# Weight rooms whose contents start 0, 16, 32 or 48 bytes in, by turns

## The chip, the cores and the metric

The kernel runs as one program on one core of a Trainium2 chip. The metric is the device time of that core in microseconds (us). Three runs of the kernel before gave 1257.59 us (median; 1257.32 to 1260.47).

A core has a matrix engine (TensorE, PE in the profile), a vector engine (VectorE, DVE), an activation engine (ScalarE, ACT), GpSimd (POOL) and SyncE (SP), which issues the DMAs. All of them work on SBUF, an on-chip memory of 128 partitions; a tile is a room with the same byte address in every partition. A matrix multiplication on PE takes two instructions: a weight load (LDWEIGHTS, shown as the engine PEld) puts the 128x128 stationary operand into the array, and a MATMUL streams the moving operand through it, one column after the other, into a PSUM bank. Both read SBUF. The weight load of the next MATMUL runs while the present MATMUL streams.

## The reference, cut to what matters

The kernel computes two decoder layers on 512 tokens of 1024 channels, each with a token mixer and a gated feed-forward network (hidden width 2816), in float32:

```
for i in range(2):
    hn = rmsnorm(h, norm_g[i, 0]) * (1 + scale) + shift        # scale, shift, gate from c @ ada_w[i, 0]
    m = s5_mixer(hn, ...) if i == 0 else fox_mixer(hn, ...)    # state space; forgetting attention
    h = h + gate * m
    hn = rmsnorm(h, norm_g[i, 1]) * (1 + scale) + shift        # from c @ ada_w[i, 1]
    a, b = split(hn @ ffn_w_up[i], 2)
    a = conv_b + sum(shifted(a, 2 - t) * conv_w[t] for t in range(3))
    h = h + gate * ((silu(a) * b) @ ffn_w_down[i])
return rmsnorm(h, final_g)
```

Most of the arithmetic is matrix products of activations with weights: 1024x1024 (three in the first mixer, four in the second), 1024x5632 and 2816x1024 in each network.

## The kernel before, in words

Channels lie on the partitions, tokens along the free dimension. A product is made in tiles: 128 output channels times 512 tokens in a PSUM bank (tile `mmp`), summed over blocks of 128 input channels (index k).

To keep float32 precision with the one-pass format float32r, each operand is stored as two rounded parts, high and low. `put_parts` makes them: ACT writes the high part (line 241), DVE subtracts it from the source and writes the low part (line 242). Each block k of a product is then three MATMULs (`mms`, line 258): high weights with the high activations, high weights with the low activations, low weights with the high activations. In an instruction's name the moving operand stands first: `mmp<-a_hi,w_lo` streams `a_hi` through the weights `w_lo`.

Weights come from HBM by `raw` (a DMA on SP's queue into a tile `raw`). `split` takes two tiles `w_hi` and `w_lo` from a pool, calls `put_parts` and returns them; `weights` does that for all blocks of one tile of output channels, in one to two splits. The rooms of `w_hi` and `w_lo` are five each (`WB`), and are used in rotation in `wpool`. The last output tiles of a network (two in the first, four in the second) take theirs from the network's own pool instead. `quarters`, in the second network, replaces a pair of products by seven smaller ones on halves (MATMULs of 256 columns, line 506); it rounds sums of weights the same way through its local `parts`. `load` inside `fox_values` splits the attention's value weights; there the weights are the moving operand (line 1275). In the second network, `sums` rounded by `form` serve as moving operands under the names `w_hi` and `w_lo` too; they lie in the network's pool.

The moving operands of the other products are `a_hi`, `a_lo` (normalized activations, one fixed room for all sub-layers), `zhi`, `zlo` (first mixer), `v` (second mixer, holding the attention's output) and `ghi`, `glo`: the gated product of a network, in groups of 11 blocks (first network, two groups through the same two rooms) or of 6 and 5 blocks (second network, four groups).

Where the rooms lie, as the program is built (bytes past a multiple of 64; every block k within a room is a multiple of 64 bytes further, so all blocks of a tile share this number):

| tile | before | with the change |
|---|---|---|
| `w_hi`, `w_lo` in `wpool` | 32 | 32, 48, 0, 16 by turns |
| `w_hi`, `w_lo` in a network's pool, as weights | 0 | 0, 16, 32, 48 by turns; those of `quarters` that hold `a22` stay at 0 |
| `a_hi`, `a_lo`, `zhi`, `zlo`, `v` | 32 | 32 |
| `ghi`, `glo`, first network | 0 | 16 (first group), 48 (second group) |
| `ghi`, `glo`, second network | 0 | 0 |
| rounded `sums` as moving operands | 0 | 0 |
| `raw` | 32 | 32 |

The rooms of `wpool` are 4096 bytes apart before and 4160 with the change, so that neighbouring rooms then differ by 64 bytes when counted past a multiple of 512. Before, all ten rooms lie 480 past a multiple of 512, as `a_hi` and `a_lo` do; `zhi`, `zlo` and `v` lie 32 past one, `ghi` and `glo` 384.

The order of the instructions on each engine is settled when the program is built. The scheduler places a tile's instructions as rooms come free.

Of the kernel before, what the change touches and what calls it, by code (L numbers as in the profile page):

```python
# [8 lines left out]
F32 = mybir.dt.float32  # L9
F32R = mybir.dt.float32r  # L10
# [7 lines left out]
P = 128  # L18
D = 1024
KT = D // P  # L20
S = 512
# [14 lines left out]
NEG = -1.0e30  # L36
HALVES = (slice(0, S // 2), slice(S // 2, S))
RAW, WB = 3, 5

GROUPS = (11, 11)  # L40
QGROUPS = (6, 5, 6, 5)
# [14 lines left out]
class Trunk:  # L56
# [6 lines left out]
    def __init__(self, tc, io, ctx):  # L63
        self.tc, self.nc, self.io, self.ctx = tc, tc.nc, io, ctx
        nc = self.nc
        pool = lambda name, bufs, **k: ctx.enter_context(tc.tile_pool(name=name, bufs=bufs, **k))
        self.const = pool("const", 1)
        self.act = pool("act", 1)
        self.wpool = pool("wpool", 3)
        self.tmp = pool("tmp", 2)  # L70
        self.small = pool("small", 2)
        self.dram = pool("dram", 1, space=DRAM)
        self.mm = pool("mm", 4, space=PSUM)
        self.aux = pool("aux", 4, space=PSUM)
        self.bg = []
        self.acc = None
        self.pending = None

        self.first = self.load_pack("first", FIRST)
        self.c = self.first["c"]  # L80
        self.ones = self.const.tile([P, P], F32, name="ones")
        nc.vector.memset(self.ones, 1.0)
        self.sc = self.const.tile([P, KT], F32, name="sc")
        nc.scalar.activation(self.sc, self.c, AF.Silu)
        self.sc32 = self.const.tile([P, KT, 32], F32, name="sc32")

        self.sel = self.const.tile([P, 6], F32, name="sel")
        nc.gpsimd.memset(self.sel, 0.0)
        for q in range(4):
            for c in (q, 4 + q % 2):  # L90
                nc.gpsimd.memset(self.sel[32 * q:32 * q + 1, c:c + 1], 1.0)
        self.par = [self.const.tile([P, 24], F32, name=f"par{i}") for i in range(4)]
        self.ga = [self.const.tile([P, KT], F32, name=f"ga{i}") for i in range(4)]
# [132 lines left out]
    def finish_norm(self, n=NORM_AFTER):  # L226

        if self.pending and n >= NORM_AFTER:
            with self.tc.issue_after(self.last_mm.ins):
                self.pending()  # L230
            self.pending = None

    def split(self, src, shape, pool=None, bufs=WB):

        hi, lo = ((pool or self.wpool).tile(shape, F32R, name=n, bufs=bufs) for n in ("w_hi", "w_lo"))
        self.put_parts(hi, lo, self.raw(shape, src))
        return hi, lo

# [5 lines left out]
    def weights(self, w, nk, *pool):  # L244

        out = []
        n8 = -(-nk // 8)
        for q in range(n8):
            a, n = q * nk // n8, (q + 1) * nk // n8 - q * nk // n8
            hi, lo = self.split(w[:, a:a + n, :], [P, n, P], *pool)  # L250
            out += [(hi[:, j, :], lo[:, j, :]) for j in range(n)]
        return out
# [217 lines left out]
    def quarters(self, pool, l, f, x, finish):  # L470

        nc = self.nc
        H, N = KT // 2, S // 2
        t1, t2 = HALVES
        a, b = (self.raw([P, KT, P], self.io["w_up"][l][2 * f + j]) for j in range(2))
        a11, a12, a21, a22 = a[:, :H], a[:, H:], b[:, :H], b[:, H:]
        c, d = (pool.tile([P, 2, H, P], F32, name="sums", bufs=2) for _ in range(2))
        sub = lambda o, u, v, op=ALU.subtract: nc.vector.tensor_tensor(o, u, v, op)
        w = {}

        def parts(src, names, *where):
            hi, lo = ((where[0] if where else self.wpool).tile(
                [P, len(names) * H, P], F32R, name=n, tag=(where[1] + n if where else n), bufs=1 if where else WB
            ) for n in ("w_hi", "w_lo"))
            self.put_parts(hi, lo, src)
            for j, n in enumerate(names):
                w[n] = hi[:, j * H:(j + 1) * H], lo[:, j * H:(j + 1) * H]

        parts(a, ("a11", "a12"))
        sub(c[:, 0], a21, a22, ALU.add)  # L490
        sub(c[:, 1], c[:, 0], a11)
        parts(c.rearrange("p n k m -> p (n k) m"), ("s1", "s2"))
        sub(d[:, 1], a11, a21)
        sub(d[:, 0], a12, c[:, 1])
        parts(d.rearrange("p n k m -> p (n k) m"), ("s4", "s3"))
        parts(a22, ("a22",), pool, "e")
        quarter = lambda k, t: tuple(v[:, k * H:(k + 1) * H, t] for v in x)
        xs = {"b11": quarter(0, t1), "b21": quarter(1, t1), "b22": quarter(1, t2)}
        for n, v in self.tx.items():
            xs[f"t{n}"] = v  # L500

        def times(o, wn, xn, first=True):
            (whi, wlo), (xhi, xlo) = w[wn], xs[xn]
            for k in range(H):
                for n, (wt, xt) in enumerate(((whi, xhi), (whi, xlo), (wlo, xhi))):
                    self.last_mm = nc.tensor.matmul(  # L506
                        o, wt[:, k], xt[:, k], start=(first and k == 0 and n == 0), stop=(k == H - 1 and n == 2),
                        skip_group_check=True,
                    )

        def copy(o):
            t = self.tmp.tile([P, N], F32, name="nm_h", bufs=4)
            nc.scalar.activation(t, o, AF.Copy)  # L513
            return t

        p1, p5 = (self.mm.tile([P, S], F32, name="mmp")[:, :N] for _ in range(2))
        p2, p4 = (self.aux.tile([P, S], F32, name="aux")[:, :N] for _ in range(2))
        oa, ob = (self.tmp.tile([P, S], F32, name="nm_t") for _ in range(2))
        times(p1, "a11", "b11")
        c1 = copy(p1)  # L520
        times(p5, "s1", "t1")
        c5 = copy(p5)
        times(p2, "a12", "b21")
        sub(oa[:, t1], p2, c1, ALU.add)
        times(p1, "s2", "t2", False)
        c2 = copy(p1)
        times(p5, "s4", "b22", False)
        sub(oa[:, t2], p5, c2, ALU.add)
        finish(2 * f, oa, slice(0, S))
        times(p4, "a22", "t4")  # L530
        c4 = copy(p4)
        times(p1, "s3", "t3", False)
        sub(ob[:, t2], p1, c5, ALU.add)
        sub(ob[:, t1], p1, c4)
        finish(2 * f + 1, ob, slice(0, S))

    def ffn(self, i, l, x, nxt, ticks=0, plain=None):

        nc, tc = self.nc, self.tc
        with tc.tile_pool(name=f"ffn{l}", bufs=1, reuse_waits="tile") as pool:  # L540
# [6 lines left out]
            keep, g = {}, {}  # L547

            def gated(m, ps, cols):
                f = m // 2  # L550
                if m % 2 == 0:
                    t = pool.tile([P, S], F32, name="conv", bufs=2 if plain else 3)
                    nc.scalar.activation(t, ps, AF.Identity, bias=cb[:, f:f + 1], scale=cw[:, 2, f:f + 1])
                    for d in (1, 2):
                        nc.vector.scalar_tensor_tensor(  # L555
                            t[:, d:], ps[:, :S - d], cw[:, 2 - d, f:f + 1], t[:, d:], op0=ALU.mult, op1=ALU.add
                        )
                    nc.scalar.activation(t, t, AF.Silu)  # L558
                    keep[f] = t
                    return  # L560
                t = keep.pop(f)
                nc.vector.tensor_tensor(t, t, ps, ALU.mult)
                q = sum(f >= n for n in first[1:])
                j = f - first[q]
                if not j:
                    tag = f"{q % 2}" if plain else ""
                    g[q] = [pool.tile([P, groups[q], S], F32R, name=n, tag=n + tag) for n in ("ghi", "glo")]
                hi, lo = g[q]
                self.put_parts(hi[:, j, :], lo[:, j, :], t)

# [157 lines left out]
class S5(Trunk):  # L728
# [34 lines left out]
    def s5_params(self, pool, tp, prm, stats):  # L763
# [19 lines left out]

        logs = [], []
        y = self.inv_root(stats, NB, log=logs[0])
        self.s5_turns(pool, co, si, logs[1])
        in_turn(*logs)
        yield y

# [41 lines left out]
        e.mul(m, m, self.mag8)  # L831
        yield last.ins

    def s5_turns(self, pool, er, ei, log):

        nc = self.nc
        H = G // 2
        LB = B.bit_length() - 1
        self.turn = pool.tile([P, LB, 3, H], F32, name="s5_turn")
        tmp = pool.tile([P, 2, 2, H], F32, name="s5_turn0")  # L840
        for k in range(LB + 2):
            o = self.turn[:, k - 2] if k >= 2 else tmp[:, k % 2]
            c, s = o[:, 0], o[:, 2 if k >= 2 else 1]
# [176 lines left out]
    def s5(self, i, nxt):  # L1020
# [5 lines left out]
        with ExitStack() as stack:  # L1026
# [3 lines left out]
            with ExitStack() as start:  # L1030
# [11 lines left out]
                with tc.manual_schedule(engines={ENG.PE, ENG.Activation, ENG.DVE, ENG.SP}):  # L1042
# [47 lines left out]
                    for k in range(KT):  # L1090
                        last_mm = nc.tensor.matmul(
                            col, w[0][:, k, :], self.par[i][:, k:k + 1], start=(k == 0), stop=(k == KT - 1)
                        )
                    shifted = self.small.tile([P, 1], F32, name="u_shift")
                    nc.scalar.activation(shifted, col, AF.Copy)
                    first = self.tmp.tile([P, L, B], F32, name="uf", tag="nm_t")
                    nc.scalar.activation(first, ps.rearrange("p (b j) -> p j b", j=L), AF.Identity, bias=shifted)
# [111 lines left out]
class Kernel(S5):  # L1209
# [32 lines left out]
    def fox_values(self, pool, x):  # L1242
# [9 lines left out]
        def load(q):  # L1252

            src = self.io["fox_v"][q - 1] if q else self.io["fox_vf"]
            n, step = (W, 4) if q else (W + NH, 3)
            out = []
            for a in range(0, KT, step):
                j = min(step, KT - a)
                hi, lo = self.split(src[:, a:a + j, :], [P, j, n])
                out += [(hi[:, i, :], lo[:, i, :]) for i in range(j)]  # L1260
            return out
# [267 lines left out]
```

## Time and profile before

| what | value |
|---|---|
| median of three runs | 1257.59 us (1257.32 to 1260.47) |
| span of the profiled execution, first to last instruction | 1254.6 us |
| mean granted TensorE clock | 0.995 |
| PE busy | 1234.3 us (98% of the span), 7464 MATMULs |
| PEld, DVE, ACT, POOL busy | 82%, 72%, 45%, 5% |
| PE's share of the chain that ended last | 94% |

The profiled execution's own time is its span, 1254.6 us; the median of the runs, which is taken with what lies around the span, is 3.0 us above it. In the profile a row of a group gives line, engine, operation, the tiles' names and sizes, the count, then busy time, mean duration and idle time before. MATMULs are pipelined: the next one starts before the end that the record gives, so the distance between starts is what one MATMUL costs PE, and the duration in the record is longer.

### The profile page before, as it was taken

How to read it: one execution, taken by the hardware profiler on the slowest of the kernel's cores; microseconds unless marked ns; L12 is line 12 of the kernel's file. 1: busy time of each engine (PE TensorE's matmuls, PEld its weight loads, DVE VectorE, ACT ScalarE, POOL GpSimd, SP SyncE). 2: the span in 40 equal slices, each digit the busy share in tenths (PEclk: the TensorE clock that was granted, in tenths of full speed). 3: DMA queues.
4: the chain of work that ended last, by engine and by line, in shares of the span. 5: the costliest groups of instructions: out<-in, count | busy, mean ns of one | idle time of the engine just before them, and what ended most of it. 6: DMA issues, size and time to landing. Idle time of an engine off the chain costs nothing.

```text
span 1254.6 us, 19342 instructions
## 1 busy us (share of the span) xinstructions
PE 1234.3 (98%) x7464; PEld 1024.5 (82%) x7464; DVE 897.5 (72%) x1610; ACT 565.8 (45%) x1043; POOL 57.5 (5%) x103
## 2 busy tenths in 40 slices
PE   7999999999999999999999999999999999999997
PEld 2566678898878778788799888878989999999987
DVE  7878887578765647666457467765899888887855
ACT  3543445334332233333334456654365555554543
POOL 0000000000000000000000224331000000000000
PEclk9999999999999999999999999999999999999999
DMA  9678667237744736545413433321213332332331
GB/s 364 231 227 259 205 196 244 99 103 234 236 137 148 236 118 221 168 147 165 141 49 103 149 117 131 133 94 53 85 60 101 120 119 82 106 118 88 102 84 68
DMA packets 73067, 183.22 MB, mean 146 GB/s; under 512 B 23079, under 2 KB 25471, under 8 KB 71951
## 3 DMA queue, kind: packets, MB, share of 16 engines
q1 hardware_dynamic: 72687, 181.46, 45.3%
q8 instruction: 59, 0.97, 0.3%
q10 hardware_dynamic: 288, 0.52, 0.1%
q14 instruction: 33, 0.27, 0.1%
HBM read 175.04 MB, written 6.92 MB: 145 GB/s over the span
## 4 chain that ended last, share of the span: by engine, by line
PE 94%; DVE 2%; DMA 1%; ACT 1%; issue 0%; SPq 0%; DVEq 0%; ACTq 0%
PE mmp L258 58%; PE mmp L506 10%; PE mmp L1110 4%; PE aux L506 4%; PE mmp L1275 2%; PE aux L916 2%; PE mmp L1139 2%; PE aux L1417 2%; PE aux L1400 1%; PE mmp L181 1%; PE aux L1005 1%; PE aux L997 1%; PE aux L1370 1%; PE mmp L1080 1%; PE mmp L1050 1%; PE aux L955 1%
## 5 line engine op out<-in xcount | busy, mean ns | idle before, releaser
L241 ACT ACTIVATE w_hi<-raw 128x1024 fp32r<-128x1024 f32 (+4 forms) x197 | 181.8, 927 | 258.2 <-PE mmp L258 211.5
L242 DVE TENSOR_TENSOR w_lo<-raw,w_hi 128x1024 fp32r<-128x1024 f32 (+4 forms) x197 | 210.1, 1070 | 92.0 <-ACT w_hi L241 88.2
L258 PE MATMUL mmp<-a_hi,w_hi 128*128 128x512 f32 (+1 forms) x624 | 235.8, 380 | 2.2 <-ACT a_hi L394 1.5
L258 PE MATMUL mmp<-a_hi,w_lo 128*128 128x512 f32 (+1 forms) x624 | 233.3, 374 | 0.0
L258 PE MATMUL mmp<-a_lo,w_hi 128*128 128x512 f32 (+1 forms) x624 | 232.7, 373 | 0.0
L258 PE MATMUL mmp<-ghi,w_hi 128*128 128x512 f32 (+1 forms) x394 | 147.2, 374 | 0.0
L258 PE MATMUL mmp<-glo,w_hi 128*128 128x512 f32 (+1 forms) x394 | 146.8, 373 | 0.0
L258 PE MATMUL mmp<-ghi,w_lo 128*128 128x512 f32 (+1 forms) x394 | 146.7, 372 | 0.0
L258 PEld LDWEIGHTS mmp<-a_hi,w_hi 128*128 128x128 f32 x624 | 117.1, 188 | 25.9 <-issue 2.6
L258 PEld LDWEIGHTS mmp<-a_hi,w_lo 128*128 128x128 f32 x624 | 117.5, 188 | 21.1 <-DVE w_lo L242 0.3
L258 PEld LDWEIGHTS mmp<-a_lo,w_hi 128*128 128x128 f32 x624 | 117.6, 188 | 19.3
L324 DVE SCALAR_TENSOR_TENSOR h<-mmp,par,h 128x512 f32<-128x512 f32 (+1 forms) x74 | 49.9, 678 | 63.9 <-PE mmp L258 63.6
L258 PEld LDWEIGHTS mmp<-ghi,w_lo 128*128 128x128 f32 x394 | 74.4, 189 | 14.1
L258 PEld LDWEIGHTS mmp<-ghi,w_hi 128*128 128x128 f32 x394 | 74.5, 189 | 13.5
L258 PEld LDWEIGHTS mmp<-glo,w_hi 128*128 128x128 f32 x394 | 74.5, 189 | 13.5
L209 DVE SCALAR_TENSOR_TENSOR ada_acc<-ada_raw,sc,ada_acc 128x1024 f32<-128x1024 f32 x49 | 62.8, 1282 | 26.6 <-DMA ada_raw<-in_ada_w 26.3
L506 PE MATMUL mmp<-w_hi 128*128 128x256 f32 x216 | 60.7, 281 | 0.2 <-ACT nm_h L513 0.2
L506 PE MATMUL mmp<-w_hi,w_lo 128*128 128x256 f32 x216 | 60.5, 280 | 0.0
L506 PE MATMUL mmp<-w_lo,w_hi 128*128 128x256 f32 x216 | 60.5, 280 | 0.0
L558 ACT ACTIVATE conv<-conv 128x512 f32<-128x512 f32 x44 | 27.5, 629 | 66.7 <-DVE conv L555 66.3
L1110 PE MATMUL mmp<-a_x,raw 128*128 128x512 f32 x112 | 54.9, 627 | 0.0
L242 DVE TENSOR_TENSOR w_lo<-sums,w_hi 128x1024 fp32r<-128x1024 f32 x40 | 48.9, 1222 | 3.8 <-ACT w_hi L241 3.7
(298 smaller groups left out, 2487.9 us busy)
## 6 DMA issues: line engine op xcount, KB each, us to landing
raw<-in_w_up SPq DMA_DIRECT2D x88, 512.0 KB, 3.4
ada_raw<-in_ada_w SPq DMA_DIRECT2D x56, 512.0 KB, 4.4
raw<-in_ada_w SPq DMA_DIRECT2D x40, 512.0 KB, 6.3
raw<-in_w_down SPq DMA_DIRECT2D x32, 384.0 KB, 3.2
raw<-in_w_down SPq DMA_DIRECT2D x32, 320.0 KB, 3.0
nf<-nfd SPq DMA_DIRECT2D x8, 1152.0 KB, 5.7
raw<-in_fox_qk SPq DMA_DIRECT2D x16, 512.0 KB, 3.7
h<-in_x SPq DMA_DIRECT2D x8, 512.0 KB, 5.6
```

Source lines behind the costliest of these rows:

```text
L209: nc.vector.scalar_tensor_tensor(acc, w, self.sc[:, k:k + 1], acc, op0=ALU.mult, op1=ALU.add)
L241: nc.scalar.activation(hi, src, AF.Copy)
L242: nc.vector.tensor_tensor(lo, src, hi.bitcast(F32), ALU.subtract)
L258: self.last_mm = self.nc.tensor.matmul(o, wt, xt[:, cols], start=(k == 0 and n == 0), stop=(k == nk - 1 and n == 2),)
L324: self.nc.vector.scalar_tensor_tensor(self.h[:, m, cols], ps, self.par[i][:, 16 + m:17 + m], self.h[:, m, cols], op0=ALU.mult, op1=ALU.add,)
L506: self.last_mm = nc.tensor.matmul(o, wt[:, k], xt[:, k], start=(first and k == 0 and n == 0), stop=(k == H - 1 and n == 2), skip_group_che ...
L558: nc.scalar.activation(t, t, AF.Silu)
L916: nc.tensor.matmul(ps[g2][:, j, cols], x[rows, a + j, r].rearrange("p c j -> p (c j)"), self.rr[rows, planes, q, :], start=(j == 0 and r = ...
L1110: nc.tensor.matmul(ps, w[m][:, k, :], x[:, k], start=(k == 0), stop=(k == KT - 1))
L1139: nc.tensor.matmul(gps[m], wt, xt[:, k], start=(k == 0 and part == 0 and xt is yhi), stop=(k == KT - 1 and part == 1))
L1275: self.last_mm = nc.tensor.matmul(ps[q, b][:, :n], xt[:, k, tb], wt, start=(k == 0 and i == 0), stop=(k == KT - 1 and i == 2),)
L1417: nc.tensor.matmul(pv[:, c * P:], self.v[:, hp, k, r].rearrange("p t d -> p (t d)"), pp[:, r, c + 3 * k:NB + 3 * k, :].rearrange("p b t -> ...
```

## The change

`PAD` is 16 elements (64 bytes). A new method `room` takes a tile that is 64 bytes longer than needed and returns a view that begins `off` elements into it. `turn_skew` steps an offset through 4, 8, 12, 0 elements: 16, 32, 48, 0 bytes. `split` and the `wpool` part of `parts` in `quarters` use that offset for both `w_hi` and `w_lo`; `weights`, `quarters` and `load` step it once per call. The rooms of the gated product in the first network begin 4 elements (first group) or 12 elements (second group) in. Two small tiles, `s5_turn0` (512 bytes) and `u_shift` (4 bytes), move from pools that live long into the pool of the start (`tp`). The instructions, their sizes and their order on the five engines are the same as before; in the first mixer one wait of DVE on a DMA's semaphore is attached to a later write of the tile `ua` than before.

```diff
+PAD = 16
...
+        self.skew = 0
...
+    def room(self, pool, shape, name, off, **k):
+
+        n = math.prod(shape[1:])
+        t = pool.tile([P, n + PAD], F32R, name=name, **k)
+        return t[:, off:off + n].rearrange("p (a b) -> p a b", b=shape[2])
+
+    def turn_skew(self):
+        self.skew = (self.skew + 4) % PAD
+
     def split(self, src, shape, pool=None, bufs=WB):
 
-        hi, lo = ((pool or self.wpool).tile(shape, F32R, name=n, bufs=bufs) for n in ("w_hi", "w_lo"))
+        hi, lo = (self.room(pool or self.wpool, shape, n, self.skew, bufs=bufs) for n in ("w_hi", "w_lo"))
         self.put_parts(hi, lo, self.raw(shape, src))
         return hi, lo
...
     def weights(self, w, nk, *pool):
 
         out = []
+        self.turn_skew()
...
+        self.turn_skew()
+
         def parts(src, names, *where):
-            hi, lo = ((where[0] if where else self.wpool).tile(
-                [P, len(names) * H, P], F32R, name=n, tag=(where[1] + n if where else n), bufs=1 if where else WB
-            ) for n in ("w_hi", "w_lo"))
+            shape = [P, len(names) * H, P]
+            if where:
+                hi, lo = (where[0].tile(shape, F32R, name=n, tag=where[1] + n, bufs=1) for n in ("w_hi", "w_lo"))
+            else:
+                hi, lo = (self.room(self.wpool, shape, n, self.skew, bufs=WB) for n in ("w_hi", "w_lo"))
...
-                    g[q] = [pool.tile([P, groups[q], S], F32R, name=n, tag=n + tag) for n in ("ghi", "glo")]
+                    new = (lambda n: pool.tile([P, groups[q], S], F32R, name=n, tag=n + tag)) if plain else (
+                        lambda n: self.room(pool, [P, groups[q], S], n, 4 + 8 * q, tag=n + tag))
+                    g[q] = [new(n) for n in ("ghi", "glo")]
...
-        self.s5_turns(pool, co, si, logs[1])
+        self.s5_turns(pool, tp, co, si, logs[1])
...
-        tmp = pool.tile([P, 2, 2, H], F32, name="s5_turn0")
+        tmp = tp.tile([P, 2, 2, H], F32, name="s5_turn0")
...
-                    shifted = self.small.tile([P, 1], F32, name="u_shift")
+                    shifted = tp.tile([P, 1], F32, name="u_shift")
...
             out = []
+            self.turn_skew()
             for a in range(0, KT, step):
```

More of the change, by code (lines that the diff above doesn't have):

```diff
@@ L832, in s5_params, with s5_turns @@
         yield last.ins
-    def s5_turns(self, pool, er, ei, log):
+    def s5_turns(self, pool, tp, er, ei, log):
         nc = self.nc
```

## The prediction

> **What bounds the kernel now.** I read the page's engine table and its chain first, then the waits of PE, then PE's groups by form, and last single stretches of PE in which nothing else happens.
>
> ```profile
> PE 1234.3 (98%) x7464; PEld 1024.5 (82%) x7464; DVE 897.5 (72%) x1610; ACT 565.8 (45%) x1043; POOL 57.5 (5%) x103
> PE 94%; DVE 2%; DMA 1%; ACT 1%; issue 0%; SPq 0%; DVEq 0%; ACTq 0%
> ...
> PE mmp L1050 <- DVE s_ring L702: 6.3, 1, 6.3
> PE mmp L258 <- ACT a_hi L394: 1.5, 2, 0.8
> ```
>
> PE is busy for 98% of the span and is 94% of the chain. Its longest wait, for the whole of a line, is the 6.3 us at the very start, and the next longest is 1.5 us. So the end is set by how fast MATMULs follow each other, and a nanosecond more or less per MATMUL goes to the end in full. The change touches nothing but addresses; what I have to price is whether the distance between two MATMULs depends on them.
>
> It does, in the trace of before. The next view takes long stretches of products whose weights lie in `wpool` (32 bytes past a multiple of 64), and gives for each kind of MATMUL the count, the duration (min/median/max) and the first and last start.
>
> ```profile
> L258 PE MATMUL mmp<-a_lo,w_hi x60: 389/389/389, 318.7 to 358.9; 128*128 128x512 f32 x60
> ...
> L258 PE MATMUL mmp<-ghi,w_hi x58: 392/397/400, 413.7 to 453.8; 128*128 128x512 f32 x58
> ...
> L258 PE MATMUL mmp<-zlo,w_hi x42: 388/388/388, 221.8 to 250.0; 128*128 128x512 f32 x42
> L258 PE MATMUL mmp<-zhi,w_lo x41: 392/392/392, 222.1 to 249.5; 128*128 128x512 f32 x41
> L258 PE MATMUL mmp<-zhi,w_hi x41: 394/394/394, 222.3 to 249.8; 128*128 128x512 f32 x41
> ```
>
> Three MATMULs stand between two starts of one kind. With `a_hi`/`a_lo` streaming the distance is (358.9 - 318.7)/59/3 = 227.1 ns; with `ghi`/`glo` (453.8 - 413.7)/57/3 = 234.5 ns; with `zhi`/`zlo` (250.0 - 221.8)/41/3 = 229.3 ns. Same instruction, same size, same engine load beside it; what differs is the place. `a_hi` shares the weights' place past a multiple of 512, `zhi` shares it past a multiple of 64 only, `ghi` lies 32 bytes off. The duration in the record is 162 to 163 ns longer than the distance (389 against 227.1, 397 against 234.5), so durations can stand in for distances: the fastest kind, 388 ns, is about 225.5 ns, the slowest, 400 ns, about 237.
>
> The same for 256 columns, in stretches of `ghi` (same place as its weights), `zhi` and `v` (same past 64), and the second network's small products (32 bytes off):
>
> ```profile
> L258 PE MATMUL mmp<-ghi,w_hi x19: 283/283/283, 633.2 to 639.7; 128*128 128x256 f32 x19
> ...
> L258 PE MATMUL mmp<-zhi,w_lo x15: 279/279/279, 253.8 to 258.7; 128*128 128x256 f32 x15
> ...
> L258 PE MATMUL mmp<-v,w_lo x16: 276/276/276, 879.1 to 884.2; 128*128 128x256 f32 x16
> ...
> L506 PE MATMUL mmp<-w_hi x4: 279/280/282, 950.3 to 951.3; 128*128 128x256 f32 x4
> ```
>
> That is 6.5/18/3 = 120.4, 4.9/14/3 = 116.7, 5.1/15/3 = 113.3 and, by the duration, about 280 - 163 = 117 ns. So at 256 columns the equal place, which is the best at 512, is the worst. At 512 columns equal places give 389 or 388/392/394 ns, one steady value per kind, while 32 bytes off runs from 392 to 400.
>
> **The change part by part.** It adds and removes no instruction on any engine, so there are two terms, how many MATMULs meet which distance, and what moves beside PE. The counts:
>
> ```profile
> L258 PE MATMUL mmp<-a_hi,w_hi 128*128 128x512 f32 x528 | 209.0, 396 | 0.7 <-ACT nm_t L1197 0.7
> L258 PE MATMUL mmp<-ghi,w_hi 128*128 128x512 f32 x310 | 123.1, 397 | 0.0
> L506 PE MATMUL mmp<-w_hi 128*128 128x256 f32 x216 | 60.7, 281 | 0.2 <-ACT nm_h L513 0.2
> L258 PE MATMUL mmp<-v,w_hi 128*128 128x512 f32 x96 | 30.3, 397 | 0.1
> L258 PE MATMUL mmp<-zhi,w_hi 128*128 128x512 f32 x48 | 18.9, 394 | 0.0
> L506 PE MATMUL mmp<-a_hi,w_hi 128*128 128x256 f32 x144 | 40.5, 281 | 0.0
> L258 PE MATMUL mmp<-a_hi,w_hi 128*128 128x256 f32 x96 | 27.2, 290 | 1.5 <-ACT a_hi L394 1.5
> L1275 PE MATMUL mmp<-w_hi,a_hi 128*128 128x256 f32 x96 | 27.1, 286 | 0.2 <-DVE v L242 0.2
> L258 PE MATMUL mmp<-ghi,w_hi 128*128 128x256 f32 x84 | 24.1, 287 | 0.0
> L1139 PE MATMUL mmp<-a_hi,w_hi 128*128 128x512 f32 x32 | 12.6, 400 | 0.0
> ```
>
> Each row but `v`'s has two sisters of the same count. At 512 columns `a_hi`/`a_lo` stream 3 x (528 + 32) = 1680 times, `ghi`/`glo` 3 x 310 = 930, `z` 144 and `v` 144 times (96 and 48). At 256 columns, 288 + 252 + 288 = 828 MATMULs of lines 258 and 1275 have equal places, and some 1500 of line 506 are a mixture near 281 ns, or 118.
>
> With turning offsets the built program pairs places as follows. `a_hi`: equal past 64 in 176 of 560 blocks (31%), 32 bytes off in 128 (23%), 16 or 48 off in 256 (46%). `ghi`: equal 29%, 32 off 21%, 16 or 48 off 50%. `z` and `v`: 17%, 33%, 50%. Even the equal ones are no longer equal past 512, since the rooms stand 4160 bytes apart; their row is `z`'s, 229.3 ns.
>
> No row shows 16 or 48 bytes off. The bounds are the two ends of all 512-column rows: 225.5 ns (388) below, 237 ns (400) above. Halfway between equal (229.3) and 32 off (234.5) would be 231.9; if any difference is as bad as 32, 234.5. I take the middle of these two, 233.2, because the nearest property these pairs share with a row is that they are unequal. Then:
>
> `a_hi` at 512: 0.31 x 229.3 + 0.23 x 234.5 + 0.46 x 233.2 = 232.3 ns, against 227.1: +5.2 ns x 1680 = +8.7 us.
> `ghi` at 512: 0.29 x 229.3 + 0.21 x 234.5 + 0.50 x 233.2 = 232.3, against 234.5: -2.2 ns x 930 = -2.0 us.
> `z` and `v` at 512: 0.17 x 229.3 + 0.33 x 234.5 + 0.50 x 233.2 = 233.0, against 229.3: +3.7 ns x 288 = +1.1 us.
> 256 columns: three quarters of the 828 go from 120.4 to 117.5, the distance of the mixed pairs, 2.9 x 0.75 x 828 = -1.8 us; the 192 of `z` and `v` go from about 115 to 117.5, +0.4 us; line 506 stays.
>
> The sum is +6.4 us on the span of 1254.6. The median of the runs stands 3.0 us above that span; I add the sum to the median: 1264.0 us.
>
> A rule of the Trainium skill speaks against all of this. TensorE: Matmul & The Clock Gate, section Step-by-step: what each phase is for, says that PE reads SBUF through two independent ports, one for the streaming operand and one for weight loads, so that loading the next weights takes nothing from the running matmul. By it the sum would be zero. The rows above differ by 7.4 ns between two places, so the trace does not bear the rule out in full, though it can't tell whether the weights or the place of the streamed tile alone makes the difference.
>
> What moves beside PE I cost at nothing, and name its cover. The parts' rounding now writes and reads at 16-byte steps on ACT and DVE:
>
> ```profile
> L242 DVE TENSOR_TENSOR w_lo<-raw,w_hi 128x1024 fp32r<-128x1024 f32 x112 | 138.8, 1241 | 64.5 <-ACT w_hi L241 61.0 <-PE mmp L1139 1.6
> L242 DVE TENSOR_TENSOR w_lo<-sums,w_hi 128x1024 fp32r<-128x1024 f32 x40 | 48.9, 1222 | 3.8 <-ACT w_hi L241 3.7
> 292.00:550.00 258.00, 258.00 (x1137) 207.53 (x1136) 162.52 (x178) 85.76 (x113) 0.00 (x0) 1.00 0.59 189
> 935.00:1255.00 320.00, 311.57 (x2154) 288.77 (x2152) 254.11 (x400) 162.72 (x260) 0.00 (x0) 0.99 0.32 99
> ```
>
> Reading a source at 0 (`sums`) or at 32 (`raw`) past 64 costs DVE 1222 or 1241 ns, no penalty for the odd place. The last two rows are stretches of the first and the second network (length, then busy PE, PEld, DVE, ACT): DVE is busy 163 of 258 and 254 of 320 us, so even 5% on it (13 us of the second) stays under PE. The rooms are as many as before, so no DMA or rounding starts later. If that cover were gone, the first late thing would be `w_lo`, for which PE's weight load waits. DVE's wait that moves in the first mixer is for a DMA into tiles used again later; its price lies between zero and one DVE operation of 0.7 us, and may be a gain as well as a loss; I take zero. `s5_turn0` and `u_shift` keep their instructions.
>
> **The rivals.**
>
> Staggering helps (the other side). The equal place at 256 columns is a bad lock (120.4 against 113.3 to 117), and the period of `z`'s three kinds (388, 392, 394) shows that 225.5 ns can be had. If 16 or 48 bytes off gives 225.5 at 512 and 113.3 at 256 columns, the sum falls by 7.7 ns on 0.46 x 1680 + 0.5 x (930 + 288) = 1382 MATMULs, 10.6 us, and by half of 4.2 ns on 2340, 4.9 us: 1264.0 - 15.5 = 1248.5 us. The place is the products of lines 258 and 506. It decides from about 225.8 ns at those pairs alone: there the sum is -3.8 us. For it: no row excludes it. Against it: `a_hi` at 227.1 is already near the least, so most products have more to lose than to gain.
>
> The pairing doesn't matter, or it washes out. If the place of the streamed tile alone sets its distance, `a_hi` stays at 227.1, and of the `ghi` products only the first network's second operand moves: 3 x 154 MATMULs at 16 or 48, between 234.5 and 227.1, so -3.7 ns x 462 = -1.7 us, 1255.9 us. For it: `ghi` is slow with the same weights. Against it: at 256 columns `ghi` at 0 and `a_hi` at 32, each with weights at its own place, both show 283 ns. The two-port rule of the skill would give 1257.6, the same case. Untested pairs near 228.6 ns also end here, by cancelling.
>
> **How the numbers follow.** A change of 0.3%, 3.8 us, is about the least that a measurement of this kernel can tell from none. The forecast (slower, 1264.0) gets 0.46: only rows with unequal places are slow ones at 512 columns. Staggering helps gets 0.28, no matter or cancelled 0.26. Its own bounds carry the forecast from 1261.4 to 1264.0 + 3.8 x 1.38 (16 and 48 off at 237) + 4.0 (no gain and a lock at 256 columns), 1273. The rivals reach down to 1248.5. I cut a little at both ends: 1249 to 1272. Faster 0.28, same 0.26, slower 0.46.
>
> **What would show it.** In the changed kernel's trace, the durations of the 512-column kinds with `a_hi` should no longer be 389 throughout but spread over some 388 to 400 from one output tile to the next, with a mean 5 ns higher; those of `ghi` should fall by about 2 ns; 283 at 256 columns should give way to about 280. PE's busy share stays at 98%, and its waits stay short. I am wrong if the 16- and 48-byte pairs run at 389 or less, or if durations stay tied to the streamed tile's name; and in another way if ACT's or DVE's rounding rows grow by more than a few per cent and PE begins to wait for `w_lo`.

## The result, and the profile after

The changed kernel takes 1261.74 us (median; 1260.81 to 1265.61), beside 1257.21 us for the kernel before on the same chip: 1.0039 times as long, 95% interval 1.0030 to 1.0047. The medians lie 4.5 us apart. The profiled execution spans 1259.3 us, 4.7 more than the 1254.6 of before, at the same mean granted clock, 0.995.

First the engine table and the chain of the page, then the chief waits of PE (engine and line that waits, what it waits for, us in all, times, longest):

```profile
PE 1238.7 (98%) x7464; PEld 1023.9 (81%) x7464; DVE 898.0 (71%) x1610; ACT 566.1 (45%) x1043; POOL 57.3 (5%) x103
PE 96%; DVE 2%; DMA 1%; ACT 1%; issue 0%; SPq 0%; DVEq 0%; ACTq 0%
...
PE mmp L1068 <- ACT nm_t L1067: 6.2, 1, 6.2
PE mmp L1098 <- DVE a_x L1084: 1.6, 1, 1.6
PE mmp L270 <- ACT a_hi L406: 1.5, 2, 0.8
```

PE is busy 4.4 us longer (1238.7 against 1234.3), with the same 7464 MATMULs, and its waits stay short: 6.2 us at the start (6.3 before), 1.6 for `a_x` (0.8 before) and 1.5 for `a_hi` (as before). DVE and ACT have not changed (898.0 and 566.1 against 897.5 and 565.8). So 4.4 of the 4.7 us are in the pace of PE.

The stretch with `a_hi` and the one with `ghi` streaming, as in the prediction (count, duration min/median/max, first and last start); line 258 of before is line 270 here:

```profile
L270 PE MATMUL mmp<-a_lo,w_hi x59: 387/393/403, 319.7 to 360.0; 128*128 128x512 f32 x59
L270 PE MATMUL mmp<-a_hi,w_lo x58: 388/392/398, 320.0 to 359.5; 128*128 128x512 f32 x58
...
L270 PE MATMUL mmp<-ghi,w_hi x55: 388/394/398, 418.1 to 455.6; 128*128 128x512 f32 x55
L270 PE MATMUL mmp<-glo,w_hi x55: 390/394/401, 418.3 to 455.8; 128*128 128x512 f32 x55
```

Before, `a_lo` showed 389/389/389; now its durations spread from 387 to 403 with a median of 393. `ghi` went the other way, from 392/397/400 to medians of 394. The two names, 8 ns apart before, are now alike.

The distance between two starts says it better than the duration in the record. I took it for every pair of neighbouring float32r MATMULs of equal size from the starts in the trace, leaving out pairs with a pause (over 250 ns at 512 columns, over 140 at 256), and averaged by the operand that streams:

```
ns from start to start     before   after   difference x count        us
512 columns  a_hi, a_lo    227.38   231.71    +4.33 x 1680         +7.27
             ghi, glo      234.27   231.75    -2.52 x  930         -2.34
             z             229.00   232.48    +3.48 x  144         +0.50
             v             229.58   232.61    +3.03 x  144         +0.44
256 columns  a_hi, a_lo    119.13   118.22    -0.91 x  936         -0.85
             weights, sums 118.43   118.12    -0.31 x 1152         -0.36
             ghi, glo      119.69   118.57    -1.12 x  252         -0.28
             v             115.42   118.57    +3.15 x   96         +0.30
             z             117.82   117.17    -0.65 x   96         -0.06
                                                       sum         +4.62
```

The sum, +4.6 us, is the whole of the 4.7 us by which the span grew, and of the 4.5 us of the medians. Nothing else of any size is left.

### The profile page after: what moved, and what is told of

The parts are those of the page before. It is cut to its first block, busy times and chain, and to the rows that moved or that the text cites. A ratio compares the mean times of both kernels' runs of the same rounds, so it can differ in the third digit from the quotient of the medians.

```text
span 1259.3 us, 19342 instructions
## 1 busy us (share of the span) xinstructions
PE 1238.7 (98%) x7464; PEld 1023.9 (81%) x7464; DVE 898.0 (71%) x1610; ACT 566.1 (45%) x1043; POOL 57.3 (5%) x103
## 4 chain that ended last, share of the span: by engine, by line
PE 96%; DVE 2%; DMA 1%; ACT 1%; issue 0%; SPq 0%; DVEq 0%; ACTq 0%
PE mmp L270 59%; PE mmp L522 10%; PE mmp L1128 4%; PE aux L522 4%; PE mmp L1294 2%; PE aux L934 2%; PE mmp L1157 2%; PE aux L1436 2%; PE aux L1419 1%; PE mmp L183 1%; PE aux L1023 1%; PE aux L1015 1%; PE aux L1389 1%; PE mmp L1068 1%; PE aux L973 1%; PE mmp L1098 1%
## 5 line engine op out<-in xcount | busy, mean ns | idle before, releaser
L270 PEld LDWEIGHTS mmp<-a_lo,w_hi 128*128 128x128 f32 x624 | 117.5, 188 | 21.1
```

The costliest lines, as they stand in the source:

```text
L270: self.last_mm = self.nc.tensor.matmul(o, wt, xt[:, cols], start=(k == 0 and n == 0), stop=(k == nk - 1 and n == 2),)
```

## The experiments

What is in question is why distances depend on places. The prediction took the difference between the weights' place and the streamed operand's, counted past 64 bytes (Theory 1 in the quoted texts). Against it stand: that the streamed operand's own place decides (Theory 2), that the difference counts, but past 256 bytes or more (Theory 3), or that the fixed distance between rooms matters rather than the offsets in them. All kernels compute the whole function. In some, `s5_turn0` is moved to the start's pool as in the change, to make space. The ratio stands against runs of the kernel before on the same chip; a is the mean distance of `a_hi` and `a_lo` at 512 columns, ghi that of `ghi` and `glo`, from starts as above. "Difference" is from here on the address of the weights minus that of the operand that streams while they are loaded; the addresses are those of the built programs.

**The weights' turns alone.** The change without its edit of the gated product's rooms (against the changed kernel):

```diff
-                    new = (lambda n: pool.tile([P, groups[q], S], F32R, name=n, tag=n + tag)) if plain else (
-                        lambda n: self.room(pool, [P, groups[q], S], n, 4 + 8 * q, tag=n + tag))
-                    g[q] = [new(n) for n in ("ghi", "glo")]
+                    g[q] = [pool.tile([P, groups[q], S], F32R, name=n, tag=n + tag) for n in ("ghi", "glo")]
```

> The change without its part on the gated product: ghi and glo begin at a multiple of 64 again, the weights still turn. Theory 1 (the forecast's: what counts is the difference between a weight and the streamed tile past 64 bytes): the products that stream ghi still meet all four differences by turns, so ghi's distance is about 232 ns all the same, and the time stays within 1 us of the changed kernel, 1261.7. Theory 2 (the streamed tile's own place counts): ghi goes back to 234 ns in the first network's 620 MATMULs at 512 columns, about 1.1 to 1.5 us slower than the changed kernel, while a_hi would have had no reason to slow down at all.

Measured: 1261.84 us, ratio 1.0046 (1.0028 to 1.0063); a 231.7, ghi 232.0. The interval contains the ratio of the whole change, and the mean distances of ghi, 232.0 and 231.8, are 0.2 us apart on 930 MATMULs: the gated product's offset adds next to nothing once the weights turn.

**The room between the rooms alone.** Every room is 64 bytes longer, but its contents begin at its start (against the run before this one):

```diff
     def turn_skew(self):
-        self.skew = (self.skew + 4) % PAD
+        self.skew = 0
```

> The rooms of the weights are 64 bytes longer, as in the change, but contents begin at 0; the gated product is as before. Every pair of weight and a_hi is then equal past 64 bytes; past 256 bytes the rooms differ by 0, 64, 128, 192. Theory 1 (64 bytes count): a_hi at 512 columns takes 229 ns at most, ghi stays at 234: +1.6 to 1.9 ns x 1680 = about +3 us, 1260. Theory 3 (the difference past 256 bytes or more counts, and the long steady stretch at 227 ns needs the same one for all rooms): a_hi rises to 231 to 232 ns, ghi falls to about 232: +7 - 2 = about +5 us, 1262. By theory 2 (own place) nothing changes, 1257.2.

Measured: 1259.68 us, ratio 1.0016 (1.0003 to 1.0029); a 230.6, ghi 232.9. Here every weight stands at the same place past 64 bytes as `a_hi`, yet the trace shows:

```profile
L270 PE MATMUL mmp<-a_hi,w_lo x59: 389/393/399, 319.8 to 359.9; 128*128 128x512 f32 x59
```

By Theory 1 the distances of `a_hi` should have been those of an equal place, 229.3 at most. 393 is the median of the whole change. The time alone could not have told: 1259.68 us is what Theory 1 had forecast (1260), by other distances. Sorted by the difference past 256 bytes, a takes 229.4 ns at 0, 232.4 at 64, 231.1 at 128 and 229.6 at 192. So Theory 1 falls: the difference counts, but in a longer period than 64 bytes. Three quarters of what a lost (3.2 of 4.3 ns) are there already with rooms that are 64 bytes longer, without turning offsets.

**The gated product's offset alone.** Only that edit, weights as before:

```diff
-                    g[q] = [pool.tile([P, groups[q], S], F32R, name=n, tag=n + tag) for n in ("ghi", "glo")]
+                    new = (lambda n: pool.tile([P, groups[q], S], F32R, name=n, tag=n + tag)) if plain else (
+                        lambda n: self.room(pool, [P, groups[q], S], n, 4 + 8 * q, tag=n + tag))
+                    g[q] = [new(n) for n in ("ghi", "glo")]
```

> The other part alone: the first network's gated product begins 16 or 48 bytes in, weights as before. All other products keep their pairs, so a_hi stays at 227 ns. ghi and glo of the first network (462 to 620 MATMULs at 512 columns) leave 234 ns: by theories 1 and 3 for about 230 to 232, which is -1 to -2 us, 1255.5 to 1256.5; by theory 2 the same.

Measured: 1255.01 us, ratio 0.9988 (0.9974 to 1.0002); a 227.4 as before, ghi 232.5. The pairs that moved take 228.5 to 232.4 ns in place of 234.3, the others still 234.3:

```profile
L265 PE MATMUL mmp<-glo,w_hi x64: 388/393/394, 412.4 to 456.0; 128*128 128x512 f32 x64
L265 PE MATMUL mmp<-ghi,w_lo x63: 392/392/393, 412.6 to 455.5; 128*128 128x512 f32 x63
```

So differences that are odd multiples of 16 bytes are no slower than the 96 bytes that they replace, though none reaches the 227.4 ns of an equal place, and 1.8 ns x 930 = 1.7 us are to be had from this part; the median fell by 1.9, though the interval just reaches 1.

**The gated product at the weights' own place.** A tile that lies ahead of `ghi` is 96 bytes longer, so that `ghi` and `glo` lie 480 past a multiple of 512 like the weights in `wpool`:

```diff
-            conv = pool.tile([P, 4, FT], F32, name="conv_wb")
+            conv = pool.tile([P, 4 * FT + 24], F32, name="conv_wb")[:, :4 * FT].rearrange("p (a b) -> p a b", b=FT)
```

> Before, with 96 more bytes ahead of everything in the networks' pools, so that ghi and glo lie 480 bytes past a multiple of 512, as the weights do; no other edit. Theories 1 and 3: ghi at 512 columns falls from 234.3 to the 227.4 ns of a_hi, 6.9 x 930 = -6.4 us; the second network's rounded sums now share the weights' place too and go from 117.9 to about 119.2 ns, 648 MATMULs, +0.8 us; together -5.6 us, about 1251.6, faster than both kernels. If equal places are no cause (a_hi being fast for another reason), ghi stays at 234 and the time at 1257.

Measured: 1253.34 us, ratio 0.9964 (0.9950 to 0.9978).

```profile
L258 PE MATMUL mmp<-glo,w_hi x54: 389/389/389, 413.8 to 449.8; 128*128 128x512 f32 x54
```

The row of `ghi` is now, to the nanosecond, that of `a_lo` before: 389 throughout, 227.3 ns. It is not the name, the data or the stage that made `ghi` slow, but its place against the weights: 7.0 ns x 930 = 6.5 us gained. Some of it is given back at 256 columns, where more pairs have equal places: 119.9 ns against 118.4 on 1152 MATMULs, 1.6 us, where 0.8 had been expected. `a_hi` and `a_lo` at 256 columns lose 0.6 us as well (119.8 ns against 119.1 on 936), though their own differences are as before. Hence 3.6 us gained and not the 5.6 of the expectation.

**The weights moved, nothing turned.** The room of `a_hi` is made 32, 64 or 192 bytes longer; `a_hi` and `a_lo` stay, and the weights and all that is allocated behind them move by as much. So the difference is a constant 32, 64 or 192 at nearly all of a's MATMULs:

```diff
-                x.append(self.act.tile([P, KT, S], F32R, name="a_hi"))
+                x.append(self.act.tile([P, KT * S + 8], F32R, name="a_hi")[:, :KT * S].rearrange("p (k t) -> p k t", t=S))
```

(8 elements for 32 bytes, 16 for 64, 48 for 192.) For 32 bytes:

> Before, with the whole of wpool (and all that lies behind it) 32 bytes later against a_hi and a_lo; nothing turns. All products that stream a_hi then have one constant difference of 32 bytes; the pairs of ghi, z and v are as before. This doubles the forecast's suspected cost without any turning. Theory 1 or 3 (the difference counts, turning only mixes differences): a_hi at 512 columns goes from 227.4 to 233 or 234 ns, +5.6 to 6.6 ns x 1680 = +9.4 to +11 us; 256 columns lose at most 0.6 us: about 1266. Theory 4 (turning itself costs, because the pace must settle anew when the rooms' places change, and a constant difference always settles at 227): no change, 1257. Theory 2 (own place of the streamed tile): no change.

Measured: 1267.4 us, ratio 1.0067 (1.0051 to 1.0084); a 233.2.

```profile
L258 PE MATMUL mmp<-a_hi,w_lo x58: 395/396/396, 325.7 to 365.6; 128*128 128x512 f32 x58
...
L258 PE MATMUL mmp<-zhi,w_hi x42: 397/397/398, 225.7 to 254.4; 128*128 128x512 f32 x42
...
L258 PE MATMUL mmp<-v,w_hi x26: 388/392/503, 850.6 to 865.1; 128*128 128x512 f32 x26
```

A constant difference of 32 bytes is worse than the whole change, and the row is steady (395 to 396), so it is not the variety of differences that costs. The `z` row I had not expected: `zhi` and its weights moved together, and yet it went from 388/392/394 to 397, while `v`, at the same place and the same difference as `z`, kept 388 to 392. For 64 bytes:

> The same with 64 bytes: a_hi equals its weights past 64 bytes, not past 256. Theory 1 (past 64 counts): a_hi at 512 columns at 227 to 229 ns, at most +2.7 us, and 256 columns as before: 1257 to 1260. Theory 3 (past 256 counts; in the run with longer rooms pairs 64 bytes off took 232.4 ns at 512 columns and 114 to 116 at 256): +5 ns x 1680 = +8.4 us, and -3 to -4 ns x 936 at 256 columns = -3.3 us, with -0.7 us where the weights stream: about +4.4 us, 1261.5, with both signs in one trace.

Measured: 1263.8 us, ratio 1.0046 (1.0031 to 1.0060); a 233.3, and `z` at 228.9 again. Theory 3 had both signs right, and its sum too small: a costs 9.9 us at 512 columns (8.4 expected) and gains 2.9 at 256 (3.3 expected), and the streamed weights gain 0.2 (0.7 expected).

```profile
L258 PE MATMUL mmp<-a_hi,w_lo x54: 393/395/398, 321.7 to 358.8; 128*128 128x512 f32 x54
```

At 64 bytes' difference the places past 64 are equal, and a is as slow as at 32. This is Theory 1's plainest miss. For 192 bytes:

> The same with 192 bytes. Theory 3, from the rows of the runs so far (z before and a_hi in the run with longer rooms, 192 off: 229.0 to 229.6 ns at 512 columns; about 116 at 256): +2 ns x 1680 = +3.3 us, -3 ns x 936 = -2.8 us, and -1.5 us where the weights stream: about -1 us, 1256. Theory 1 makes no difference between this and 64 bytes.

Measured: 1257.29 us, ratio 0.9995 (0.9984 to 1.0005); a 229.2.

```profile
L258 PE MATMUL mmp<-a_hi,w_hi x59: 392/392/392, 319.8 to 359.6; 128*128 128x512 f32 x59
```

192 is the difference of `z` and `v` in the kernel before, counted past 256 bytes (past 512 theirs is 448), and a takes their distance (229.0 and 229.6) with it. What a loses at 512 columns (1.8 ns x 1680 = 3.1 us) it nearly gets back at 256: 117.4 against 119.1 ns on 936 MATMULs, and 117.5 against 118.4 on 1152, together 2.7 us. The expectation had 3.3 us lost and 4.3 gained back.

**All moved together.** A tile that is allocated ahead of all others is 32 bytes longer; weights, activations, `z`, `v` and the gated product all lie 32 bytes further, with the differences of the kernel before:

```diff
-        self.sc32 = self.const.tile([P, KT, 32], F32, name="sc32")
+        self.sc32 = self.const.tile([P, KT * 32 + 8], F32, name="sc32")[:, :KT * 32].rearrange("p (k c) -> p k c", c=32)
```

> A tile allocated before all others is made 32 bytes longer, so that the activations, the weights, the first mixer's z and the gated product all lie 32 bytes further (the weights and a_hi at 0 past a multiple of 512, z at 64); every difference between a weight and the operand that streams past it is that of the kernel before. Theory 3 (differences alone decide): 1257 us within 0.2%, a_hi at 512 columns 227 ns (389), z 229 ns (388, 392, 394). Rival (the place itself counts too, which would explain why z went to 233 ns where the weights alone were moved by 32 bytes): z at 397 or so, +0.6 us on its 144 MATMULs, and if the same holds for a_hi, up to +6 ns on 1680 MATMULs, 1267 us.

Measured: 1257.18 us, ratio 0.9997 (0.9983 to 1.0010); a 227.4, ghi 234.3, `z` 229.1.

```profile
L258 PE MATMUL mmp<-a_lo,w_hi x64: 389/389/398, 317.8 to 361.9; 128*128 128x512 f32 x64
...
L258 PE MATMUL mmp<-zhi,w_hi x46: 388/388/397, 220.9 to 251.8; 128*128 128x512 f32 x46
```

A shift of all places by 32 bytes changes none of these distances, while the same shift of the weights alone costs a 5.8 ns: what counts at 512 columns is not the place of the one operand or the other, but the two together. The 397 of `z` with the weights 32 bytes further is not explained by its place either: here `z` and its weights lie at the very same places, and run at 388 to 394 but for a few.

**The best places found, put together.** `ghi` and `glo` as in the run above, and operands of 256 columns 64 or 192 bytes (past 256) off their weights, but for those of `a_hi`, `a_lo` and the attention's value weights: the rooms of `sums` are 96 bytes longer, those of `a22` begin 64 bytes in, the first network's `glo` is 192 bytes longer:

```diff
-            t = pool.tile([P, H, N], F32, name="sums", bufs=2)
+            t = pool.tile([P, H * N + 24], F32, name="sums", bufs=2)[:, :H * N].rearrange("p (k t) -> p k t", t=N)
...
+                a = where[0].tile([P, n + 16], F32R, name="w_hi", tag=where[1] + "w_hi", bufs=1)[:, 16:]
...
-            conv = pool.tile([P, 4, FT], F32, name="conv_wb")
+            conv = pool.tile([P, 4 * FT + 24], F32, name="conv_wb")[:, :4 * FT].rearrange("p (a b) -> p a b", b=FT)
...
+                        pool.tile([P, n + (0 if plain or name == "ghi" else 48)], F32R, name=name, tag=name + tag)[:, :n]
```

> Before, with constant places chosen by the runs' rows: ghi and glo share the weights' place past 512 where they stream 512 columns; the second network's rounded sums lie 64 bytes under the weights they meet at 256 columns, and the last weights of each network 192 bytes off ghi. Theory 3: ghi at 512 columns 234.3 to 227.3 (-6.3 us), sums at 256 columns from 118.4 to 114 in some 860 MATMULs (-3.5 us), the last weights from 119.7 to 116 (-0.9 us): about -10 us, 1247, faster than both kernels. Theory 1: only the first term, less 1 us lost on the sums: 1252.

Measured: 1246.64 us, ratio 0.9907 (0.9892 to 0.9921): faster than both kernels. From the groups by form (count, then busy us and mean ns of one, then idle time before):

```profile
L258 PE MATMUL mmp<-ghi,w_hi 128*128 128x512 f32 x310 | 120.9, 390 | 0.0
...
L510 PE MATMUL mmp<-w_hi,w_lo 128*128 128x256 f32 x216 | 59.7, 276 | 0.0
```

The same groups took 397 and 280 before, and 395 and 281 with the change. ghi gives 7.2 ns x 930 = 6.7 us, the streamed weights and sums at 256 columns 2.7 ns x 1152 = 3.1 us (115.8 against 118.4), `ghi` at 256 columns 0.5; together 10.3 of the 10.8 us measured.

All runs in one table. "By distances" is the sum of (distance - distance before) x count, made as in the section above; "by medians" is the difference of the two medians:

```
                            a      ghi    by distances   by medians
the change                231.7  231.8       +4.6           +4.5
weights' turns alone      231.7  232.0       +4.7           +4.9
64 bytes between rooms    230.6  232.9       +3.1           +2.8
gated offset alone        227.4  232.5       -1.5           -1.9
gated at weights' place   227.4  227.3       -3.9           -3.6
weights 32 bytes further  233.2  234.3       +9.3           +9.9
weights 64 bytes further  233.3  234.3       +7.0           +6.3
weights 192 bytes further 229.2  234.3       +0.6           -0.2
all 32 bytes further      227.4  234.3       -0.1           +0.1
best places together      227.4  227.1      -10.2          -10.8
```

The distances carry every run to within 0.8 us.

## Why the prediction was right or wrong

**The direction and the bound.** Right: slower, 4.5 us where 6.4 were summed. PE stays at 98%, its waits stay short, and the pace of MATMULs, set by how weights and streamed operand lie to each other, carries the loss. What was wrong is the rule by which places were compared.

**The term of `a_hi` at 512 columns.** Forecast +5.2 ns and +8.7 us, measured +4.3 ns and +7.3 us. Its basis failed: the step that sorts pairs by their difference past 64 bytes. Sorted so, the changed kernel shows no order:

```
difference past 64 bytes:     0      16      32      48
a_hi, a_lo (ns)             230.8   232.0   232.6   231.7
ghi, glo (ns)               231.5   232.0   232.2   231.3
```

The equal pairs were taken at 229.3 from `z`'s row and measure 230.8 and 231.5; those 16 or 48 off were taken at 233.2 and lie near 232. `z`'s row was read as "equal past 64"; in truth it is the row of one difference, 192, which is a good one among the multiples of 64. In the changed kernel, a at 0, 192 and 240 bytes past 256 takes 229.1 to 229.8 ns, and every other difference 230.6 to 233.5. That forecast and result agree as closely as they do is partly luck. The equal pairs were 1.5 and 2.2 ns slower than taken, all others 1.2 to 2.3 ns faster, and these errors partly offset each other in the mean.

**The terms of `ghi`, and of `z` and `v`.** Forecast -2.0 and +1.1 us, measured -2.3 and +0.9. The mechanism, that turning weights take `ghi` out of a bad constant difference, is shown: 234.3 goes to 232.0 with the weights' turns alone. The part that moves `ghi` itself makes a gain only while the weights stand still.

**256 columns.** Forecast -1.8 + 0.4 = -1.4 us, measured -0.85 - 0.36 - 0.28 + 0.30 - 0.06 = -1.25 us. (The gain of `z` and `v` was summed with the wrong last digit: 2.5 ns x 192 is 0.5, not 0.4.) Line 506 stayed, as was taken, but by two terms that cancel: -0.4 us for `a_hi` and `a_lo`, +0.4 for the sums. That equal places are the worst here holds: 119.9 ns with nearly all equal, 113.9 for streamed weights at 64 bytes' difference in the run with longer rooms.

**The cover.** DVE's and ACT's rounding was costed at nothing, and that is what it took. The rows are those of `put_parts`, after:

```profile
L253 DVE TENSOR_TENSOR w_lo<-sums,w_hi 128x1024 fp32r<-128x1024 f32 x40 | 48.9, 1221 | 4.3 <-ACT w_hi L252 4.0
L252 ACT ACTIVATE w_hi<-raw 128x1024 fp32r<-128x1024 f32 (+4 forms) x197 | 181.9, 928 | 263.7 <-PE mmp L270 219.6
L253 DVE TENSOR_TENSOR w_lo<-raw,w_hi 128x1024 fp32r<-128x1024 f32 (+4 forms) x197 | 209.9, 1069 | 91.8 <-ACT w_hi L252 87.8
```

Before, their means were 1222, 927 and 1070 ns. Rooms that begin at 16, 32 or 48 by turns cost these engines nothing that shows.

**The rival that staggering helps.** Wrong for this change, since no pair 16 or 48 off reached 225.5 ns on the mean. What the rival named as a bad lock is one, though: at 256 columns the equal place, and for `ghi` the constant difference. Choosing places one by one gains 10.8 us.

**The rival that the pairing doesn't matter.** Ruled out. With `a_hi` fixed and the weights 32 bytes further, its MATMULs take 5.8 ns more; with both moved by 32 they take nothing more. So it is neither place alone but the two together. The rule of the Trainium skill that I set beside it (TensorE: Matmul & The Clock Gate, Step-by-step: what each phase is for: two independent ports, so that a weight load takes nothing from the running matmul) does not hold to this precision here: the same pair of instructions takes 227.4 or 233.3 ns by the difference of their addresses. What the two then share isn't shown.

## What to carry to other kernels

When PE is busy throughout and its operands are streamed back to back, read the distance between MATMUL starts for each kind of operand; if two kinds of one size differ, compare the addresses of the weights and of the streamed tile. Put them at a difference that measures well, here 0 (counted past 512 bytes) for 512 columns and 64 (past 256) for 256 columns, by lengthening a tile ahead of them, and keep the rooms of a rotation at one spacing that preserves it. Offsets that turn give every product the average of good and bad differences: a gain for a product that stood badly, a loss for one that stood well.

## What the runs showed of the hardware that was not expected

Distances settle into patterns of whole steps. In float32r at 512 columns the steady mean distances are 226.7 ns (389 throughout) and 233.3 (397 throughout), 34 and 35 times 6.67 ns; at 256 columns 120.0 and 113.3, 18 and 17 times. `ghi` before runs a pattern that repeats after seven MATMULs and 1640 ns, 246 such steps. What has this step isn't shown.

The best difference at 512 columns is the worst at 256: 227.4 and 119.9 ns at 0; 233.3 and 116.0 (a) or 114.6 (streamed weights) at 64.

One and the same difference can run at two paces. The `z` and `v` rows with the weights 32 bytes further (397; 388 to 392) have equal places and an equal difference. At 256 columns `z` and `v` even change roles between two kernels with the same differences, first before, then with all moved by 32 bytes:

```profile
L258 PE MATMUL mmp<-zhi,w_hi x15: 279/279/279, 253.5 to 258.5; 128*128 128x256 f32 x15
...
L258 PE MATMUL mmp<-v,w_hi x32: 276/276/276, 878.9 to 884.1; 128*128 128x256 f32 x32
```

```profile
L258 PE MATMUL mmp<-zhi,w_hi x15: 276/276/276, 253.9 to 258.7; 128*128 128x256 f32 x15
L258 PE MATMUL mmp<-v,w_hi x30: 279/279/394, 878.8 to 884.2; 128*128 128x256 f32 x29, 128*128 128x512 f32 x1
```

Nor does it take a shift: in the run with the gated product at the weights' own place, those of `z` and `v` are untouched, and yet `v` at 256 columns goes from 115.4 to 117.8 ns. A pace, once taken, is kept for tens of MATMULs, as if the way in had chosen it. It also fits that a takes 227.4 ns where its difference is always 0, but 229.4 on the mean where 0 comes among other differences: there 226 to 228 and 233 to 236 stand side by side. That the way in decides is argued, not shown, and what sets it stays open. So does whether the difference counts past 256 or past 512 bytes: with 64 bytes between rooms, a takes 228.4 ns at multiples of 512 and 230.7 at 256 beside one, but both hold distances of either pace. For 256 speaks that 192 (a, moved) and 448 (`z` and `v`, before) run alike, 229.2 ns against 229.0 and 229.6.

What DVE and ACT do beside PE shows no influence on this pace in the one stretch looked at. In the kernel before, `a_lo` keeps 389/389/389 over a stretch in which DVE is busy 25 of 40 us and ACT 14 (stretch, length, then busy us of PE, PEld, DVE, ACT, POOL with their counts, granted clock, DMA share, GB/s):

```profile
319.00:359.00 40.00, 40.00 (x178) 33.14 (x177) 25.07 (x27) 14.22 (x18) 0.00 (x0) 1.00 0.58 191
```
